# A hybrid decoder layer on one core: its prologue in another order

## The chip, the core and the metric

One core of a Trainium2 chip runs the whole program. The metric is device microseconds of one execution, from the chip. TensorE multiplies, VectorE and ScalarE do elementwise work, GpSimd fills constants, and SyncE issues the loads. Each engine works through its own list in order and waits for others at semaphores.

## What is computed

The reference is one layer of a decoder trunk over 256 tokens of 1024 channels: x is normalised, scaled and shifted by vectors made from the conditioning c, and multiplied by one wide matrix; three token mixers, gates and an output product follow. The change touches what stands ahead of the first products, the first two lines and the start of the third:

```python
shift, scale, gate = jnp.split(c @ w_ada[l] + b_ada[l], 3, axis=-1)
h = rmsnorm(x, norm_pre[l]) * (1.0 + scale[:, None]) + shift[:, None]
proj = h @ w_in[l] + b_in[l]
...
merged = (g[:, :, 0] * (y_a @ w_branch[l, 0]) + g[:, :, 1] * (y_b @ w_branch[l, 1])
          + g[:, :, 2] * (y_c @ w_branch[l, 2]))
out = merged @ w_out[l]
x = x + gate[:, None] * rmsnorm(out, norm_post[l])
```

## The kernel before

All is float32. A large product is made of three: each operand is split into a high part, rounded to the fast format (`hi`, a cast on ScalarE), and the rest (`lo`, a subtraction on VectorE); `hi*hi`, `hi*lo` and `lo*hi` are summed in PSUM. One weight tile is 128 x 1024; its split is one pass on ScalarE and one on VectorE.

**The prologue** (lines 325 to 500). `heat(n)` is n products of ones, whose result nobody reads. c, one value per partition and block of 128, is spread by eight products with an identity (`ps_cb`, line 348) into `cb`, 128 equal rows of 1024, which VectorE copies out of PSUM in two halves. x lies with tokens on partitions; ScalarE squares it with a running sum (`ss`), TensorE transposes it in 16 blocks (`ps_x`, `flip`), and the reciprocal root `r` of each token is refined on VectorE (`x_norm`), spread by two products (`ps_rx`) and read into `rrow` with a factor -0.5. xn is the transposed x times `rrow`. Its first half is made at once (`evac_x`), its second is copied out raw and multiplied by `rrow` later, at k = 3 and k = 5 of the loop.

**The wave** (the loop `for k in range(KT)`, from line 506). Step k holds channels 128 k to 128 k + 127. It needs the scale and the shift of these channels: `ada_dot` (line 491) is one pass of VectorE over 128 x 1024 of w_ada times `cb`, with a sum per partition, and there are two of them for each k. From them come the columns `a` and `b` (three small VectorE steps); ScalarE makes `h_hi` and `h_f` = a * xn + b, VectorE `h_lo`; the two weight tiles of the step are split; then TensorE runs 48 products of 128 x 256 into eight PSUM banks, which all eight steps share. A weight buffer is free for the load of step k+2 when VectorE is done with it: four buffers of 1 MB are in turn, two for each step.

**The order of the rest.** Every instruction is issued in the order in which the Python code makes it. After the wave this order is set by a planner, the class `Loom`: it charges each engine an estimated time for each instruction and lets generators (attention, convolution, gates) step in between the large products when its clock says that their operands are due. What is charged in the prologue therefore moves where later small work stands.

The names in the trace: `w` is the PSUM of the wave, `ps_f` and `ps_t` that of the later large products; `w_raw`, `w_hi`, `w_lo` the weight tile and its parts; `a_raw` a pair of rows of w_ada; `acol`, `bcol` the columns a and b. Nearly all instructions are recorded at line 174, the helper that issues them.

## Time and profile before

| | us |
|---|---|
| median of 3 runs (504.64 to 504.78) | 504.76 |
| the profiled execution | 505.05 |
| its span, first to last instruction | 503.3 |
| TensorE busy | 491.2 (98%) |
| VectorE busy | 433.3 (86%) |
| ScalarE busy | 306.7 (61%) |
| first product of the wave | 14.88 |
| first product after the wave | 62.65 |
| last large product | 495.56 |

The span is what the timeline covers; the rest of the execution's 505.05 us lies around it. TensorE's busy time is that of products that overlap, and their ends are modelled: where the pace of products matters, the distance from one start to the next is the better number. A float32 product of 128 columns leaves two records on TensorE, a transpose and a product of the fast format one. In the table of stages, the clock column says what share of full speed TensorE was granted.

### The profile page before, as it was taken

What the parts mean: (1) busy time and instruction counts of PE and PEld (TensorE: products, weight loads), DVE (VectorE), ACT (ScalarE), POOL (GpSimd) and SP (SyncE); (2) the same over time, 40 slices, a digit from 0 to 9 for tenths busy, and PEclk for the clock granted to TensorE, in tenths of its full rate; (3) what the DMA queues carried; (4) which work ended last, traced back from release to release, by engine and by line L of the source; (5) the groups of instructions that cost most, each with busy time, mean ns of one, the idle gap of its engine ahead of it and who ended that gap; (6) DMA issues with size and microseconds to landing.
All of it is one profiled execution on the core that took longest, in us unless ns stands there. A gap on an engine that the chain in (4) does not pass through costs nothing.

```text
span 503.3 us, 8482 instructions
## 1 busy us (share of the span) xinstructions
PE 491.2 (98%) x3221; PEld 436.5 (87%) x3221; DVE 433.3 (86%) x871; ACT 306.7 (61%) x520; POOL 7.3 (1%) x41
## 2 busy tenths in 40 slices
PE   7999999999999999999999999999999999999994
PEld 7999999789878989978899799997888788888883
DVE  3999889999999999999799997679998986656745
ACT  3646665335365868969767874666666834454442
POOL 5000000000000000000000000000000000000000
PEclk9999999999999999999999999999999999999998
DMA  8999965784787242443423526555277596655402
GB/s 309 331 364 331 411 267 198 302 318 180 262 316 255 85 169 85 168 139 114 167 85 133 191 72 233 178 195 205 98 300 312 189 349 247 236 215 195 168 0 83
DMA packets 18496, 106.38 MB, mean 211 GB/s; under 512 B 2188, under 2 KB 2584, under 8 KB 8344
## 3 DMA queue, kind: packets, MB, share of 16 engines
q1 hardware_dynamic: 18312, 105.82, 56.8%
q8 instruction: 25, 0.41, 0.3%
q14 instruction: 15, 0.12, 0.1%
q10 hardware_dynamic: 144, 0.03, 0.0%
HBM read 104.78 MB, written 1.06 MB: 210 GB/s over the span
## 4 chain that ended last, share of the span: by engine, by line
PE 87%; DVE 6%; ACT 2%; DMA 1%; issue 1%; POOL 1%; DVEq 0%; SPq 0%; POOLq 0%; ACTq 0%
PE ps_f L174 37%; PE ps_t L174 30%; PE ps_out L174 4%; PE ps_o L174 3%; DVE w_lo L174 2%; PE w L174 2%; PE ps_s L174 2%; DVE a_raw L174 2%; PE ps_c L174 2%; DMA w_raw<-in_wave_dram 1%; PE ps_p L174 1%; ACT w_hi L174 1%; PE ps_n L174 1%; PE ps_qk L174 1%; PE ps_cb L174 1%
## 5 line engine op out<-in xcount | busy, mean ns | idle before, releaser
L174 DVE TENSOR_TENSOR w_lo<-w_raw,w_hi 128x1024 fp32r<-128x1024 f32 x148 | 179.7, 1219 | 38.4 <-ACT w_hi L174 37.1
L174 ACT CAST w_hi<-w_raw 128x1024 fp32r<-128x1024 f32 x148 | 154.4, 1045 | 73.3 <-PE ps_t L174 52.5
L174 PE MATMUL ps_f<-h_hi,w_hi 128*128 128x256 f32 x512 | 130.8, 292 | 0.0
L174 PE MATMUL ps_f<-h_lo,w_hi 128*128 128x256 f32 x512 | 126.2, 283 | 0.0
L174 PEld LDWEIGHTS ps_f<-h_hi,w_hi 128*128 128x128 f32 x512 | 98.0, 191 | 2.4 <-issue 1.5
L174 PEld LDWEIGHTS ps_f<-h_lo,w_hi 128*128 128x128 f32 x512 | 98.1, 192 | 1.1 <-issue 0.7
L174 DVE SCALAR_TENSOR_TENSOR acc<-u,p_sb,acc 128x226 f32<-128x226 f32 (+28 forms) x232 | 92.8, 459 | 2.0 <-ACT acc L174 2.0
L174 PE MATMUL ps_f<-h_hi,w_lo 128*128 128x256 f32 x512 | 75.2, 287 | 0.0
L174 PEld LDWEIGHTS ps_f<-h_hi,w_lo 128*128 128x128 f32 x512 | 66.6, 191 | 2.5 <-issue 1.3
L174 PE MATMUL ps_t<-w_hi,h_hi 128*128 128x512 f32 x144 | 57.1, 397 | 0.2 <-DVE gs L174 0.2
L174 PE MATMUL ps_t<-w_hi,h_lo 128*128 128x512 f32 x144 | 56.2, 391 | 0.0
L174 PE MATMUL ps_t<-w_lo,h_hi 128*128 128x512 f32 x144 | 44.6, 391 | 0.0
L174 PEld LDWEIGHTS ps_t<-w_hi,h_hi 128*128 128x128 f32 x144 | 27.0, 188 | 6.8 <-issue 0.8
L174 ACT ACT_TABLE_LOAD x24 | 30.8, 1283 | 1.6 <-PEq L1493 1.2
L174 PEld LDWEIGHTS ps_t<-w_lo,h_hi 128*128 128x128 f32 x144 | 26.9, 188 | 5.7
L174 PEld LDWEIGHTS ps_t<-w_hi,h_lo 128*128 128x128 f32 x144 | 27.1, 188 | 5.3
L174 PE MATMUL w<-h_lo,w_hi 128*128 128x256 f32 x128 | 31.4, 283 | 0.0
L174 PE MATMUL w<-h_hi,w_lo 128*128 128x256 f32 x128 | 31.3, 282 | 0.0
L174 DVE SCALAR_TENSOR_TENSOR a_raw<-a_raw,cb 128x1024 f32<-128x1024 f32 x24 | 28.6, 1218 | 0.0
L174 PEld LDWEIGHTS w<-h_hi,w_lo 128*128 128x128 f32 x128 | 24.5, 191 | 0.0
L174 PEld LDWEIGHTS w<-h_lo,w_hi 128*128 128x128 f32 x128 | 24.5, 191 | 0.0
L174 ACT ACTIVATE pm<-pm,mx 128x16 f32<-128x16 f32 (+2 forms) x48 | 18.9, 397 | 2.9 <-DVE mx L174 2.9
(259 smaller groups left out, 695.0 us busy)
## 6 DMA issues: line engine op xcount, KB each, us to landing
w_raw<-in_wgrp_dram SPq DMA_DIRECT2D x50, 1024.0 KB, 5.1
w_raw<-in_wbr_dram SPq DMA_DIRECT2D x12, 1024.0 KB, 4.9
a_raw<-in_wada_dram SPq DMA_DIRECT2D x16, 512.0 KB, 7.0
w_raw<-in_wave_dram SPq DMA_DIRECT2D x16, 512.0 KB, 6.5
w_raw<-in_w_dram SPq DMA_DIRECT2D x8, 1024.0 KB, 4.8
a_raw<-in_wada_dram SPq DMA_DIRECT2D x4, 1024.0 KB, 4.8
w_raw<-in_wout_dram SPq DMA_DIRECT2D x4, 1024.0 KB, 4.8
vb_mg<-in_vbias_dram SPq DMA_DIRECT2D x3, 512.0 KB, 6.1
```

The lines of the kernel that those rows point to most:

```text
L174: inst = self.pin(fn(*args, **kw))
```

## The change

The prologue and the first two steps of the wave are written in another order, and some of their work is done in another way.

- The heats are 10 and 4 (before 5, 3 and 6).
- c is spread in two halves, each behind the two transposes of one half of x (blocks 0 and 1). VectorE copies one half of `cb`, ScalarE the other.
- The scale of k = 0 comes from TensorE: eight products of 128 x 128 blocks of w_ada, stored in another layout, with c as a broadcast column (`scale_mm`, `ps_a`), four before and four behind the spreading of r. `ada_dot` makes the shift of k = 0, as before.
- Blocks 2 to 7 of x are multiplied by r where they lie, with tokens on partitions (ScalarE one half, VectorE the other: 128 x 768 each), then transposed in 12 blocks, and read out with a factor -0.5 by ScalarE (`evac_late`, three passes). The two late multiplications at k = 3 and 5 are gone.
- In steps 0 and 1 `h_hi` is made on VectorE, the first weight tile is loaded and split in halves, and the scale dot of k = 1 stands in step 0.

```diff
@@ -61,7 +61,7 @@
 CATCH = 7
 BRANCHES = ((2, "c"), (0, "a"), (1, "b"))
 AHEAD = {2: ((0, 1), ()), 0: ((0,), (1,)), 1: ((0, 1), ())}
-HEAT = (5, 3, 6)
+HEAT = (10, 4)
 LEAD = 2
 BANKS = dict(mm=3, sd=3, ml=2)
 BIG, MID = 10, 3
@@ -342,12 +342,6 @@
     ident = const.tile([128, 128], F32, name="ident")
     make_identity(nc, ident)
     cb = const.tile([128, D], F32, name="cb")
-    ps_cb = [bank("ps_cb", "sd") for _ in range(2)]
-    for i in range(2):
-        for j in range(4):
-            mm(ps_cb[i][:, 128 * j:128 * j + 128], pc("c", 4 * i + j).broadcast_to([128, 128]), ident, True, True)
-        dve.tensor_copy(cb[:, 512 * i:512 * i + 512], ps_cb[i])
-        drop(ps_cb[i])
 
     def causal(o, rows_ge_cols, fill):
         pool.affine_select(out=o, in_=o, compare_op=OP.is_ge, fill=fill, base=0,
@@ -462,22 +456,34 @@
 
     xn = bigt("xn")
     xnf = xn.rearrange("p k s -> p (k s)")
-    ptr = [bank("ps_x", kind) for kind in ("mm", "sd", "ml", "ml")]
     ss, r, v = [work.tile([128, 2], F32, name=f"x{n}", bufs=1) for n in "srv"]
     rrow = const.tile([128, S], F32, name="rrow")
 
-    def evac_x(i):
-        dve.tensor_tensor(xn[:, 2 * i:2 * i + 2], ptr[i].rearrange("p (k s) -> p k s", k=2),
-                          rrow[:, None, :].broadcast_to([128, 2, S]), op=OP.mult)
+    def evac_late(i):
+        act.mul(xn[:, 2 * i:2 * i + 2], ptr[i].rearrange("p (k s) -> p k s", k=2), -0.5)
         drop(ptr[i])
+
+    def evac_x(i, j):
+        dve.tensor_tensor(xn[:, 2 * i + j], ptr[i][:, S * j:S * j + S], rrow, op=OP.mult)
+        if j:
+            drop(ptr[i])
+
+    ptr = [bank("ps_x", "ml")]
+    ps_cb = [bank("ps_cb", "sd") for _ in range(2)]
+
+    def flip_x(k, t):
+        flip(ptr[k // 2][:, 256 * (k % 2) + 128 * t:256 * (k % 2) + 128 * t + 128], x_sb[:, t, 128 * k:128 * k + 128])
 
     for t in range(2):
         act.activation(xnf[:, D * t:D * t + D], x_sb[:, t], AF.Square, accum_out=ss[:, t:t + 1])
-        for k in range(KT):
-            flip(ptr[k // 2][:, 256 * (k % 2) + 128 * t:256 * (k % 2) + 128 * t + 128],
-                 x_sb[:, t, 128 * k:128 * k + 128])
+        for k in range(2):
+            flip_x(k, t)
+        for j in range(4):
+            mm(ps_cb[t][:, 128 * j:128 * j + 128], pc("c", 4 * t + j).broadcast_to([128, 128]), ident, True, True)
+    dve.tensor_copy(cb[:, 0:512], ps_cb[0])
+    drop(ps_cb[0])
     act.activation(r, ss, AF.Sqrt, bias=eps, scale=1.0 / D)
-    heat(HEAT[1])
+    dve.tensor_scalar(v, ss, 1.0 / D, 1e-6, op0=OP.mult, op1=OP.add)
 
     def x_norm():
         dve.reciprocal(r, r)
@@ -487,6 +493,9 @@
         ps = bank("ps_rx")
         for t in range(2):
             mm(ps[:, 128 * t:128 * t + 128], r[:, t:t + 1].broadcast_to([128, 128]), ident, True, True)
+        late = [x_sb[:, t, 256:] for t in range(2)]
+        act.mul(late[0], late[0], r[:, 0:1])
+        dve.tensor_scalar(late[1], late[1], r[:, 1:2], None, op0=OP.mult)
         act.mul(rrow, ps[:, 0:S], -0.5)
         drop(ps)
 
@@ -502,52 +511,90 @@
     bcol = const.tile([128, 8], F32, name="bcol")
 
     kinds = [k for k in BANKS for _ in range(BANKS[k])]
-    banks = [bank(f"w0_{f}", kinds[f]) for f in range(8)]
+    raws_, wraws = [], []
     for k in range(KT):
-        raw = rawt([128, 2, D], "a_raw")
-        wraw = rawt([128, 2, 1024], "w_raw")
-        for i in range(2):
-            loom.load(nc.sync, raw[:, i], wada[k, :, i])
-        for i in range(2):
-            loom.load(nc.sync, wraw[:, i], wave0[k, :, 1024 * i:1024 * i + 1024])
-        if k == 0:
-            dve.tensor_scalar(v, ss, 1.0 / D, 1e-6, op0=OP.mult, op1=OP.add)
-        ada_dot(raw[:, 0], 8 + k)
-        if k == 0:
-            x_norm()
-        ada_dot(raw[:, 1], k)
-        if k == 0:
-            evac_x(0)
-        a, b = acol[:, k:k + 1], bcol[:, k:k + 1]
-        dve.scalar_tensor_tensor(a, adac[:, 8 + k:9 + k], 1.0, pc("b_ada", 8 + k), op0=OP.add, op1=OP.add)
-        dve.tensor_tensor(b, adac[:, k:k + 1], pc("b_ada", k), op=OP.add)
-        dve.tensor_tensor(a, a, pc("npre", k), op=OP.mult)
+        for j in range(k, k + 2 if k == 0 else k + 1 if k > 1 else k):
+            raw = rawt([128, 2, D], "a_raw")
+            wraw = rawt([128, 2, 1024], "w_raw")
+            raws_.append(raw)
+            wraws.append(wraw)
+            for i in range(2):
+                loom.load(nc.sync, raw[:, i], wada[j, :, i])
+            cuts = (0, 512, 1024, 2048) if j < 2 else (0, 1024, 2048)
+            flat = wraw.rearrange("p a b -> p (a b)")
+            for c0, c1 in zip(cuts, cuts[1:]):
+                loom.load(nc.sync, flat[:, c0:c1], wave0[j, :, c0:c1])
+        raw, wraw = raws_[k], wraws[k]
         hi = [ringt(his, [128, 1024], "w_hi", "hi", HIS, F32R) for _ in range(2)]
         lo = [ringt(los, [128, 1024], "w_lo", "lo", LOS, F32R) for _ in range(2)]
         h = h_f[:, k]
-        act.copy(hi[0], wraw[:, 0])
-        if 4 < k < CATCH:
+        a, b = acol[:, k:k + 1], bcol[:, k:k + 1]
+        if k == 0:
+            act.copy(cb[:, 512:], ps_cb[1])
+            drop(ps_cb[1])
+            ps_a = bank("ps_a")
+
+            def scale_mm(js):
+                for j in js:
+                    mm(ps_a[:, 0:128], raw[:, 0, 128 * j:128 * j + 128], pc("c", j).broadcast_to([128, 128]),
+                       j == 0, j == KT - 1)
+
+            scale_mm(range(4))
+            x_norm()
+            scale_mm(range(4, 8))
+            ada_dot(raw[:, 1], 0)
+            evac_x(0, 0)
+            mods = ps_a[:, 0:1], adac[:, 0:1]
+        else:
+            if k > 1:
+                ada_dot(raw[:, 0], 8 + k)
+            ada_dot(raw[:, 1], k)
+            mods = adac[:, 8 + k:9 + k], adac[:, k:k + 1]
+        dve.scalar_tensor_tensor(a, mods[0], 1.0, pc("b_ada", 8 + k), op0=OP.add, op1=OP.add)
+        dve.tensor_tensor(a, a, pc("npre", k), op=OP.mult)
+        dve.tensor_tensor(b, mods[1], pc("b_ada", k), op=OP.add)
+        if k == 0:
+            drop(ps_a)
+            ptr += [bank("ps_x", kind) for kind in ("sd", "ml", "sd")]
+            for t in range(2):
+                for j in range(2, KT):
+                    flip_x(j, t)
+            heat(HEAT[1])
+        if k < 2:
+            act.copy(hi[0][:, 0:512], wraw[:, 0, 0:512])
+            dve.tensor_scalar(h_hi[:, k], xn[:, k], a, b, op0=OP.mult, op1=OP.add)
+            act.copy(hi[0][:, 512:], wraw[:, 0, 512:])
+        else:
+            act.copy(hi[0], wraw[:, 0])
+            if 4 < k < CATCH:
+                act.copy(hi[1], wraw[:, 1])
+            act.activation(h_hi[:, k], xn[:, k], AF.Identity, scale=a, bias=b)
+        act.activation(h, xn[:, k], AF.Identity, scale=a, bias=b)
+        if k == 0:
+            evac_late(1)
+        if k < 5 or k >= CATCH:
             act.copy(hi[1], wraw[:, 1])
         if k == 0:
-            heat(HEAT[2])
-        act.activation(h_hi[:, k], xn[:, k], AF.Identity, scale=a, bias=b)
-        act.activation(h, xn[:, k], AF.Identity, scale=a, bias=b)
-        if k < 5 or k >= CATCH:
-            act.copy(hi[1], wraw[:, 1])
+            evac_late(2)
+            evac_late(3)
         if k == KT - 3:
             act.activation(warm, warm, AF.Sigmoid)
-        dve.tensor_tensor(lo[0], wraw[:, 0], hi[0], op=OP.subtract)
-        dve.tensor_tensor(h_lo[:, k], h, h_hi[:, k], op=OP.subtract)
+        if k < 2:
+            dve.tensor_tensor(lo[0][:, 0:512], wraw[:, 0, 0:512], hi[0][:, 0:512], op=OP.subtract)
+            dve.tensor_tensor(h_lo[:, k], h, h_hi[:, k], op=OP.subtract)
+            dve.tensor_tensor(lo[0][:, 512:], wraw[:, 0, 512:], hi[0][:, 512:], op=OP.subtract)
+            if k == 0:
+                evac_x(0, 1)
+        else:
+            dve.tensor_tensor(lo[0], wraw[:, 0], hi[0], op=OP.subtract)
+            dve.tensor_tensor(h_lo[:, k], h, h_hi[:, k], op=OP.subtract)
         if k == 0:
-            evac_x(1)
-            for i in range(2, 4):
-                act.copy(xn[:, 2 * i:2 * i + 2], ptr[i].rearrange("p (k s) -> p k s", k=2))
-                drop(ptr[i])
+            ada_dot(raws_[1][:, 0], 9)
         dve.tensor_tensor(lo[1], wraw[:, 1], hi[1], op=OP.subtract)
-        if k in (3, 5):
-            c = xn[:, k + 1:k + 3]
-            dve.tensor_tensor(c, c, rrow[:, None, :].broadcast_to([128, 2, S]), op=OP.mult)
         drop(raw, wraw)
+
+        if k == 0:
+            banks = [bank(f"w0_{f}", kinds[f]) for f in range(8)]
 
         def w0(f, j, w, x, start, stop):
             c = (f % 4) * 256 + j * 128
@@ -1431,6 +1478,7 @@
     a["xtok"] = cc(x.reshape(2, 128, D).transpose(1, 0, 2).reshape(128, 2 * D))
     wa = arr(w_ada)[0].T.reshape(3, 8, 128, D)
     pairs = [np.stack([wa[1, k], wa[0, k]], 1) for k in range(8)]
+    pairs[0] = np.stack([ktiles(wa[1, 0].T), wa[0, 0]], 1)
     pairs += [np.stack([wa[2, k], wa[2, k + 1]], 1) for k in range(0, 8, 2)]
     a["wada"] = cc(np.stack(pairs))
     o = OFF["ba"], OFF["bb"]
```

Where instructions stand now, in each engine's list. TensorE, from the start to the first products of the wave (`w`); before:

```order
L174 MATMUL ps_heat<-ones 128x128 x5
L174 MATMUL ps_cb<-ident,p_sb 128x128 x8
L174 MATMUL ps_x<-ident,x_sb 128x128 x16
L174 MATMUL ps_heat<-ones 128x128 x3
L174 MATMUL ps_rx<-ident,xr 128x128 x2
L174 MATMUL ps_heat<-ones 128x128 x6
L174 MATMUL w_0_194<-h_hi,w_hi 128x256 x2
```

The same place of the changed kernel (`ps_a` is the scale of k = 0):

```order
L174 MATMUL ps_heat<-ones 128x128 x10
L174 MATMUL ps_x<-ident,x_sb 128x128 x2
L174 MATMUL ps_cb<-ident,p_sb 128x128 x4
L174 MATMUL ps_x<-ident,x_sb 128x128 x2
L174 MATMUL ps_cb<-ident,p_sb 128x128 x4
L174 MATMUL ps_a<-p_sb,a_raw 128x128 x4
L174 MATMUL ps_rx<-ident,xr 128x128 x2
L174 MATMUL ps_a<-p_sb,a_raw 128x128 x4
L174 MATMUL ps_x<-ident,x_sb 128x128 x12
L174 MATMUL ps_heat<-ones 128x128 x4
L174 MATMUL w_0_257<-h_hi,w_hi 128x256 x2
```

The spreading of r (`ps_rx`) now stands ahead of 12 of the 16 transposes, and these stand between it and the wave.

VectorE, from the copy of `cb` to the first `w_lo`; before:

```order
L174 COPY cb<-ps_cb 128x512 x2
L174 TENSOR_SCALAR xv<-xs 128x2
L174 SCALAR_TENSOR_TENSOR a_raw,adac<-a_raw,cb 128x1024
L174 RECIPROCAL xr<-xr 128x2
L174 TENSOR_TENSOR xv<-xv,xr 128x2 x2
L174 SCALAR_TENSOR_TENSOR xr<-xv,xr 128x2
L174 SCALAR_TENSOR_TENSOR a_raw,adac<-a_raw,cb 128x1024
L174 TENSOR_TENSOR xn<-ps_x,rrow 128x512
L174 SCALAR_TENSOR_TENSOR acol<-adac,p_sb 128x1
L174 TENSOR_TENSOR bcol<-adac,p_sb 128x1
L174 TENSOR_TENSOR acol<-acol,p_sb 128x1
L174 TENSOR_TENSOR w_lo<-w_raw,w_hi 128x1024
```

The same place of the changed kernel:

```order
L174 COPY cb<-ps_cb 128x512
L174 TENSOR_SCALAR xv<-xs 128x2
L174 RECIPROCAL xr<-xr 128x2
L174 TENSOR_TENSOR xv<-xv,xr 128x2 x2
L174 SCALAR_TENSOR_TENSOR xr<-xv,xr 128x2
L174 TENSOR_SCALAR x_sb<-x_sb,xr 128x768
L174 SCALAR_TENSOR_TENSOR a_raw,adac<-a_raw,cb 128x1024
L174 TENSOR_TENSOR xn<-ps_x,rrow 128x256
L174 SCALAR_TENSOR_TENSOR acol<-ps_a,p_sb 128x1
L174 TENSOR_TENSOR acol<-acol,p_sb 128x1
L174 TENSOR_TENSOR bcol<-adac,p_sb 128x1
L174 TENSOR_SCALAR h_hi<-xn,acol,bcol 128x256
```

One of the two dots ahead of `acol` is gone, a pass over 768 columns of x stands ahead of the other, and `h_hi` is VectorE's.

TensorE behind the wave, at the end of a group of `ps_f` and the start of the next of `ps_t` (`ps_b`, `ps_c` and `ps_r` are small products of the gates and of the attention's compression); before:

```order
L174 MATMUL ps_b<-lf,upper 128x4
L174 MATMUL ps_b<-lf,ones 128x4
L174 MATMUL ps_b<-lf,upper 128x4
L174 MATMUL ps_f<-h_hi,w_lo 128x256 x8
L174 MATMUL ps_c_1002<-w_raw,ckb 32x256 x8
L174 MATMUL ps_r<-ident,acols 4x128 x2
L174 MATMUL ps_t<-w_hi,h_hi 128x512
L174 MATMUL ps_t<-w_hi,h_lo 128x512
```

The same place of the changed kernel:

```order
L174 MATMUL ps_f<-h_hi,w_lo 128x256 x8
L174 MATMUL ps_t<-w_hi,h_hi 128x512
L174 MATMUL ps_t<-w_hi,h_lo 128x512
L174 MATMUL ps_c_1020<-w_raw,ckb 32x256 x8
L174 MATMUL ps_r<-ident,acols 4x128 x2
```

The planner put `ps_c` and `ps_r` two large products later; such moves stand all through the rest of the program. ScalarE's list has 20 table loads in place of 24.

## Rows read from the trace of the kernel before

**Rows 1.** Stages: us, busy PE, PEld, DVE, ACT, POOL (records), clock, DMA share, GB/s.

```profile
0.00:14.88 14.88, 11.34 (x64) 10.89 (x64) 5.99 (x16) 6.05 (x11) 6.38 (x32) 1.00 0.86 326
14.88:62.65 47.77, 47.16 (x385) 46.44 (x385) 43.88 (x81) 29.04 (x40) 0.00 (x0) 1.00 0.97 356
62.65:280.00 217.35, 217.31 (x1615) 194.65 (x1613) 209.56 (x517) 145.13 (x299) 0.92 (x9) 1.00 0.52 190
```

**Rows 2.** Timeline, TensorE: start, us, engine, line, operation, shape, count [idle before <-releaser].

```profile
1.05 2.50 PE L174 MATMUL ps_heat<-ones 128*128 128x128 f32 x10 [1.05 <-POOL eps L322]
5.29 3.75 PE L174 MATMUL ps_cb<-ident,p_sb 128*128 128x128 f32 x16 [1.73 <-POOL mrow L856]
8.83 2.84 PE L174 MATMUL ps_x<-ident,x_sb 128*128 128x128 f32 x16
11.51 0.83 PE L174 MATMUL ps_heat<-ones 128*128 128x128 f32 x6
12.18 0.61 PE L174 MATMUL ps_rx<-ident,xr 128*128 128x128 f32 x4
...
14.88 0.39 PE L174 MATMUL w<-h_hi,w_hi 128*128 128x256 f32 x1 [0.75 <-ACT h_hi L174]
```

**Rows 3.** The same, two short pieces of the transposes.

```profile
9.05 1.70 PE L174 MATMUL ps_x<-ident,x_sb 128*128 128x128 f32 x7
...
10.86 0.71 PE L174 MATMUL ps_x<-ident,x_sb 128*128 128x128 f32 x5
```

**Rows 4.** Timeline, VectorE from 9 to 14.2 us.

```profile
9.80 1.23 DVE L174 SCALAR_TENSOR_TENSOR a_raw<-a_raw,cb 128x1024 f32<-128x1024 f32 x1
...
10.95 0.16 DVE L174 RECIPROCAL xr<-xr 128x2 f32<-128x2 f32 x1
...
11.62 1.22 DVE L174 SCALAR_TENSOR_TENSOR a_raw<-a_raw,cb 128x1024 f32<-128x1024 f32 x1
...
13.24 0.69 DVE L174 TENSOR_TENSOR xn<-ps_x,rrow 128x512 f32<-128x512 f32 x1 [0.40 <-ACT rrow L174]
13.85 0.15 DVE L174 SCALAR_TENSOR_TENSOR acol<-adac,p_sb 128x1 f32<-128x1 f32 x1
...
14.18 1.23 DVE L174 TENSOR_TENSOR w_lo<-w_raw,w_hi 128x1024 fp32r<-128x1024 f32 x1
```

**Rows 5.** Timeline, ScalarE from 5 to 14.3 us.

```profile
5.00 1.06 ACT L174 ACTIVATE xn<-x_sb 128x1024 f32<-128x1024 f32 x1 [2.26 <-DMA x_sb<-in_xtok_dram]
...
12.83 0.38 ACT L174 ACTIVATE rrow<-ps_rx 128x256 f32<-128x256 f32 x1 [5.03 <-PE ps_rx L174]
...
14.23 0.60 ACT L174 ACTIVATE h_hi<-xn,bcol,acol 128x256 fp32r<-128x256 f32 x1
```

**Rows 6.** Timeline, TensorE at the steps k = 4 and k = 6.

```profile
38.27 0.28 PE L174 MATMUL w<-h_hi,w_lo 128*128 128x256 f32 x1
39.02 0.39 PE L174 MATMUL w<-h_hi,w_hi 128*128 128x256 f32 x1 [0.47 <-ACT h_hi L174]
...
50.62 0.28 PE L174 MATMUL w<-h_hi,w_lo 128*128 128x256 f32 x1
51.04 0.51 PE L174 MATMUL w<-h_hi,w_hi 128*128 128x256 f32 x2
```

**Rows 7.** Timeline, VectorE, the rescaling ahead of k = 4 and one step.

```profile
35.09 0.69 DVE L174 TENSOR_TENSOR xn<-xn,rrow 128x512 f32<-128x512 f32 x1
35.69 1.22 DVE L174 SCALAR_TENSOR_TENSOR a_raw<-a_raw,cb 128x1024 f32<-128x1024 f32 x1
...
41.57 1.22 DVE L174 SCALAR_TENSOR_TENSOR a_raw<-a_raw,cb 128x1024 f32<-128x1024 f32 x1
```

**Rows 8.** Timeline, ScalarE, the second weight tile of k = 6.

```profile
49.43 1.05 ACT L174 CAST w_hi<-w_raw 128x1024 fp32r<-128x1024 f32 x1 [1.03 <-DMA w_raw<-in_wave_dram]
```

**Rows 9.** SyncE's loads of the second a_raw; time to landing (tile view).

```profile
4.03 1.47 SPq L204 DMA_DIRECT2D a_raw<-in_wada_dram  x2
...
DMA to landing us min/median/max: 9.1/9.1/9.2
```

## The prediction, made before the changed kernel ran

> **What bounds the kernel now.** I read the table by stage first [rows 1]. From 62.65 us on TensorE is busy 217.31 of 217.35 us, so nothing there shortens the run unless TensorE arrives earlier. Between 14.88 and 62.65 it is busy 47.16 of 47.77 us: that is the first product of the network, eight steps over k of 48 products each, which I call the wave. Before 14.88 it runs nothing that the reference asks for as a large product. So the change is worth two things: how much earlier the first wave product starts, and how many of the wave's small gaps close. The rest rides along, if the later order keeps TensorE fed; the 7.7 us behind the last product stay.
>
> Then the timeline of TensorE in the prologue [rows 2]: 64 records from 1.05 us, with a hole before the spreading of c (it starts at 5.29), and a hole of 0.75 us before the first wave product, which waits for h_hi. A product of 128 float32 columns leaves two records, a transpose one. Their pace has two values. The 16 records of ps_cb take 8.83 - 5.29 = 3.54 us, 0.221 each; seven transposes from 9.05 take 1.70 us with the tail of the last, and inside a run I take 0.213. The six heats at 11.51 take 0.67 us, 0.112 each. So TensorE starts at the lower of its levels (1.2 GHz) and has the higher (2.4 GHz) by 10.86; those seven are still slow, five from 10.86 take only 0.71 us [rows 3]. The rise lies near 10.65, amid transposes, after work without a hole since 5.29. (The clock column reads 1.00 from the start; here the pace must tell.)
>
> Then VectorE and ScalarE in the same stretch [rows 4, 5]. The dot with the scale row cannot start before c is spread (9.80), the one with the shift row stands behind the small norm steps (11.62), rrow comes at 12.83 because its products stand behind 16 transposes and three heats, then xn (13.24), a and b (13.85 to 14.18), and h_hi on ScalarE (14.23, 0.60 long). That chain sets 14.88.
>
> **The change part by part.**
>
> *TensorE's prologue.* It becomes 20 heat records (ten heats), 2 + 2 transposes, 16 of c, 16 new ones (ps_a, the scale of k=0 by eight products), 4 of rrow, 12 transposes, 8 heat records: 80 in place of 64. With ten heats the hole before 5.29 fills: ten records take 2.50 us, ten more 2.13, so the heats reach to about 5.5; the first half of x is there at 5.00 [rows 5]. From 1.05 on TensorE has no hole unless an operand is late. At 0.213 throughout, the first wave product could start at 1.2 + 80 x 0.213 = 18.2; if the clock rises at T, it is 9.6 + 0.474 T (each record after T takes 0.112 instead of 0.213). T is the unknown. Its ends: 10.65 as before (start 14.65), and 5.5, the end of the heats (12.2). No row shows a rise after so long an early run. I take 7.5, nearer to the early end, because the run without a hole starts 4.2 us earlier than before: start 13.15.
>
> *What the first product waits for, at T = 7.5.* The first half of c is spread at about 7.75. VectorE copies it (0.69, as the 512-wide step at 13.24 [rows 4]) to 8.5, one small step to 8.6, four small norm steps (11.62 - 10.95 = 0.67) to 9.3; r is there. ScalarE copies the other half of cb meanwhile. VectorE scales the second 768 columns of x: no row shows this operation; it is between the 512-wide step (0.69) and a 1024-wide one (1.23), I take 0.9: 10.2. The shift dot, 1.15 from start to start, to 11.35; xn of 256 columns, 0.4 by the 0.69 of 512, to 11.75; a and b, 14.18 - 13.85 = 0.33, to 12.1; h_hi, now on VectorE and 256 wide as well, 0.4, to 12.5. The dot with the scale row (1.15) and half of the first xn step are gone from this path. rrow does not hold it: its products stand behind four ps_a products (9.6 to 10.05), ScalarE scales its own part of x from 9.5 to 10.4 (a 1024-wide pass takes 1.06 [rows 5]) and writes rrow (0.38) by 10.8. w_hi, now in halves, is ready too. So h_hi is 0.6 us ahead of TensorE's own queue, whose last members are 12 transposes and 4 heats (20 x 0.112 = 2.2 us); those transposes wait for the scaled x (10.4) and are reached at about 10.95. The eight ps_a products cost TensorE 1.8 us and the four late heats 0.9 us, and both are on the path in this count. **Term 1: 14.88 to 13.15, 1.7 us gained** (bounds: 0.2 and 2.7).
>
> *The wave.* 384 products at 0.12 us are 46.1 us; it takes 47.77. The largest holes are at 39.02 (0.75 us from the product before, start to start, in place of 0.12) and 51.04 (0.42) [rows 6]. The first comes from the rescaling of xn on VectorE (0.69, 0.60 of it in the step) [rows 7]: with x scaled ahead, both rescalings go. The second comes from a weight tile that lands late, ScalarE waits for it to 49.43 [rows 8]: this stays. The other steps start about 0.1 late each, since the loop of VectorE and ScalarE takes 41.57 - 35.69 = 5.88 us [rows 7] and 48 products take 5.76. Does the new start outrun VectorE? After h_hi it has two half w_lo and h_lo (14.05), xn (14.45), the scale dot of k=1, brought forward, (15.6; its row of w_ada lands 9.1 us after 4.03, at 13.1 [rows 9]), w_lo (16.75), one dot (17.9), a, b and h_hi (18.65); TensorE is at k=1 at 18.9. At k=2 it is 24.6 against 24.7. From there the 5.88 loop is again 0.1 longer than TensorE's step. So 0.6 is sure, 0.1 to 0.2 in each of the first two steps likely, the full 1.6 not. **Term 2: 0.9 us gained** (0.5 to 1.5).
>
> *Costs that I put at nothing.* Three loads in place of two for k=0 and 1: all are issued far ahead of their bytes, and the same bytes pass. evac_late on ScalarE: three 512-wide passes, half of 1.06 us each, beside TensorE's first step, the last done near 15.3, when the sixth bank is needed at 13.15 + 3.1 = 16.3; without that cover up to 0.5. Banks that the transposes hold are otherwise free by then.
>
> *The later order.* The planner times the rest by what it charged so far, so small products and ScalarE's work stand elsewhere among the large ones. The work is the same, apart from 20 table loads in place of 24. TensorE idles 0.04 us of 217 after the wave [rows 1], so there is nothing to win, and VectorE is busy 209.56 of those 217.35, so there is something to lose. Bounds: 0 and about 2 us lost; I take 0.
>
> *Sum.* The profiled run took 505.05 us (span 503.3, 1.75 around it). 505.05 - 1.7 - 0.9 = 502.45. The median, 504.76, lies 0.29 lower: **502.15**.
>
> **The rivals.**
>
> *A. The start hardly moves.* T stays near 10.65, or VectorE's path is late because cb is spread at the lower clock: the start is 14.65 and only the wave's gain remains, up to 1.4 then, since VectorE gets ahead: 503.2 to 504.1. For it: the clock rose only at 10.65 before, though the first heats ran at 1.05. Against: what then ran without a hole from 5.29 now does so from 1.05. Chance 0.14.
>
> *B. The later part takes it back.* VectorE at 96% is next to TensorE; where the new order brings TensorE to a product whose operand VectorE has not made, it waits. 1 to 2.6 us back: 503.2 to 504.8. Against: VectorE's prologue shortens as well, by a dot, two rescalings and half of the cb copies. Chance 0.12.
>
> *C. The clock is still low when the wave should start.* Then the 80 records are a loss: there are 16 more than before, and by the formula each us of delay of the rise costs 0.47 us. With the wave's 1.4 the gain is used up at a start of 16.3, so T = 14.1; from T = 16.2 on it is slower by over 0.2%, and with no rise before the wave it starts at 18.2, 3.4 us later: 504.76 + 3.4 - 1.4 = 506.8, and wave products at the lower pace on top. For it: the last records before the wave are 12 transposes and only 8 of heat, where 6 + 4 + 12 stood after the transposes. Against: [rows 3], the clock rose while transposes ran. The Trainium skill, "TensorE: Matmul & The Clock Gate", section "Part 4: PE-mode transpose", says that a transpose does not count as activity in the way that lets TensorE have its full clock. By that page 16 of the 80 records do nothing for the clock and the last 12 may let it go, which is this rival; the trace, in which it rose with eight transposes just behind it and more running, does not support it but does not exclude it, as products stood before them. Chance 0.05.
>
> *D. More than forecast.* T near 5.5 and the whole 1.6 us of the wave: below 500.9. Chance 0.05.
>
> **How the numbers follow.** The forecast, 500.9 to 503.2, has 0.64; A 0.14, B 0.12, C 0.05, D 0.05. The range 500.7 to 504.2 takes in A and most of B, and leaves out C, a part of D and the end of B. About 0.2% (1.0 us) is what a measurement can tell from no change: the line lies at 503.75. Faster: 0.64 + 0.05 + half of A and B, 0.82. Same: the other half, 0.13. Slower: C, 0.05.
>
> **What would show it.** In the profile after: heats, transposes and c without a hole from 1.05, and the pace falling to 0.112 near 7.5 (term 1); the first wave product near 13.15 behind heat, not behind h_hi; the next steps near 18.9 and 24.7 (term 2), no hole at the fifth step, the wave's end near 60.0 in place of 62.65; after it, TensorE idle under 0.5 us up to its last product. It is wrong if the pace stays at 0.213 past 10.65 (A, C), if the first product waits for VectorE (the 768-wide step or the dot mis-sized), or if TensorE shows idle time behind VectorE after the wave (B).

## The result, and the profile after

The changed kernel takes 502.11 us in the median of four runs (501.86 to 502.75), the kernel before 504.75 in four beside it (504.64 to 504.78): a ratio of 0.9947, 95% interval 0.9934 to 0.9961. It is 2.6 us faster; the forecast was 502.15. Further down, one run of e8_x_unscaled, its profiled one (1253.91 us), and one of e11_half_ada (985.67) ran far slower throughout than the others of their kernels; all medians are of the other runs.

| | before | after |
|---|---|---|
| the profiled execution, us | 505.05 | 502.75 |
| pace of TensorE doubles at | 10.73 | 5.0 |
| first product of the wave | 14.88 | 12.49 |
| length of the wave | 47.77 | 47.15 |
| first product after the wave | 62.65 | 59.64 |
| from there to the last large product | 432.91 | 433.58 |

The profiled executions differ by 2.30: 2.39 gained at the start, 0.62 in the wave, 0.67 lost behind it, and 0.04 around them. After's profiled run is the slowest of its four. The three stages of after, in the columns of [rows 1]:

```profile
0.00:12.49 12.49, 11.05 (x81) 10.86 (x81) 5.18 (x16) 8.34 (x15) 6.38 (x32) 1.00 0.83 297
12.49:59.64 47.15, 47.11 (x387) 46.43 (x386) 42.55 (x81) 28.14 (x39) 0.00 (x0) 1.00 1.00 388
59.64:277.00 217.36, 216.81 (x1612) 194.32 (x1611) 211.94 (x525) 140.29 (x296) 0.92 (x9) 1.00 0.51 190
```

DMA engines were busy 0.97 of the wave before and are busy 1.00 of it now. Behind the wave TensorE idles 0.55 us (217.36 less 216.81) where it idled 0.04. TensorE's prologue, in the columns of [rows 2]:

```profile
1.05 4.37 PE L174 MATMUL ps_heat<-ones 128*128 128x128 f32 x20 [1.05 <-POOL eps L322]
5.26 0.38 PE L174 MATMUL ps_x<-ident,x_sb 128*128 128x128 f32 x2
5.47 1.06 PE L174 MATMUL ps_cb<-ident,p_sb 128*128 128x128 f32 x8
...
8.03 1.16 PE L174 MATMUL ps_a<-p_sb,a_raw 128*128 128x128 f32 x8 [0.39 <-DMA a_raw<-in_wada_dram]
9.03 0.61 PE L174 MATMUL ps_rx<-ident,xr 128*128 128x128 f32 x4
9.47 1.06 PE L174 MATMUL ps_a<-p_sb,a_raw 128*128 128x128 f32 x8
10.37 1.47 PE L174 MATMUL ps_x<-ident,x_sb 128*128 128x128 f32 x12
11.68 1.06 PE L174 MATMUL ps_heat<-ones 128*128 128x128 f32 x8
12.49 0.96 PE L174 MATMUL w<-h_hi,w_hi 128*128 128x256 f32 x6
```

The heats fill the time from 1.05 to 5.26, and their pace changes inside them: 17 records up to 4.7 us lie 0.213 apart, the records from 5.03 on 0.11. The first wave product starts behind heat, with no wait of its own. VectorE ahead of it, as in [rows 4]:

```profile
8.53 0.62 DVE L174 TENSOR_SCALAR x_sb<-x_sb,xr 128x768 f32<-128x768 f32 x1
9.37 1.23 DVE L174 SCALAR_TENSOR_TENSOR a_raw<-a_raw,cb 128x1024 f32<-128x1024 f32 x1 [0.21 <-DMA a_raw<-in_wada_dram]
...
10.52 0.42 DVE L174 TENSOR_TENSOR xn<-ps_x,rrow 128x256 f32<-128x256 f32 x1
...
11.30 0.41 DVE L174 TENSOR_SCALAR h_hi<-xn,acol,bcol 128x256 fp32r<-128x256 f32 x1
```

`h_hi` ends at 11.71, 0.78 before TensorE comes to it. TensorE at k = 4, which answers to [rows 6]:

```profile
35.81 0.28 PE L174 MATMUL w<-h_hi,w_lo 128*128 128x256 f32 x1
36.03 0.62 PE L174 MATMUL w<-h_hi,w_hi 128*128 128x256 f32 x3
```

The distance there is 0.22; before it was 0.75. What TensorE waits for behind the wave (engine, tile, releaser: us in all, times, longest):

```profile
PE ps_c L174 <- DMA w_raw<-in_w_dram: 0.4, 1, 0.4
PE ps_t L174 <- DVE w_lo L174: 0.3, 1, 0.3
PE ps_t L174 <- DVE gs L174: 0.2, 1, 0.2
PE ps_b L174 <- DVE lf L174: 0.2, 1, 0.2
```

The kernel before has the two `ps_t` rows alone; `ps_c` and `ps_b` are new, 0.6 us together, nearly all of the 0.67. Whether the new order brings them is looked at below.

### The profile page after: what moved, and what is told of

Its sections match the earlier page's. It is cut to its first block, busy times and chain, and to the rows that moved or that the text cites. A ratio compares the mean times of both kernels' runs of the same rounds, so it can differ in the third digit from the quotient of the medians.

```text
span 501.0 us, 8523 instructions
## 1 busy us (share of the span) xinstructions
PE 491.0 (98%) x3237; PEld 436.4 (87%) x3237; DVE 431.8 (86%) x871; ACT 303.1 (61%) x519; POOL 7.3 (1%) x41
## 4 chain that ended last, share of the span: by engine, by line
PE 83%; DVE 11%; DMA 2%; issue 2%; ACT 1%; SPq 0%; DVEq 0%; ACTq 0%
PE ps_f L174 30%; PE ps_t L174 28%; PE w L174 9%; PE ps_out L174 4%; DVE w_lo L174 4%; DVE acc L174 3%; PE ps_o L174 3%; PE ps_s L174 2%; PE ps_p L174 1%; DMA a_raw<-in_wada_dram 1%; DMA w_raw<-in_w_dram 1%; PE ps_qk L174 1%; PE ps_n L174 1%; PE ps_c L174 1%; DVE cm L174 1%
## 5 line engine op out<-in xcount | busy, mean ns | idle before, releaser
L174 DVE TENSOR_TENSOR w_lo<-w_raw,w_hi 128x1024 fp32r<-128x1024 f32 (+1 forms) x150 | 180.0, 1205 | 40.6 <-ACT w_hi L174 39.2
L174 ACT CAST w_hi<-w_raw 128x1024 fp32r<-128x1024 f32 (+1 forms) x150 | 154.9, 1034 | 81.9 <-PE ps_t L174 53.3
L174 PE MATMUL ps_t<-w_hi,h_hi 128*128 128x512 f32 x144 | 58.2, 404 | 0.2 <-DVE gs L174 0.2
L174 DVE SCALAR_TENSOR_TENSOR a_raw<-a_raw,cb 128x1024 f32<-128x1024 f32 x23 | 27.4, 1218 | 0.2 <-DMA a_raw<-in_wada_dram 0.2
```

Of the source, the lines that this page charges most:

```text
L174: inst = self.pin(fn(*args, **kw))
```

## Experiments

A ratio is to the kernel before on the same chip, in 9 to 17 runs per group (medians 504.69 to 504.86). An interval reaches about 0.6 us to either side, so smaller differences of two medians are open unless the traces show their place. There is one profile of each kernel. The kernels ran in three groups, each on its own chip: e0 to e3; e7, e8, e10 and e11; e5, e6, e12 and e13.

| | median us | ratio, interval | first product | wave |
|---|---|---|---|---|
| e0_after | 502.28 | 0.9944 (0.9932 to 0.9956) | 12.57 | 46.77 |
| e1_pin | 502.12 | 0.9942 (0.9930 to 0.9954) | 12.46 | 47.08 |
| e2_heat5 | 503.01 | 0.9959 (0.9945 to 0.9973) | 14.43 | 46.24 |
| e3_before_heat10 | 503.42 | 0.9973 (0.9963 to 0.9983) | 13.84 | 47.61 |
| e7_scale_vector | 502.59 | 0.9951 (0.9936 to 0.9965) | 12.76 | 47.63 |
| e8_x_unscaled | 503.04 | 0.9961 (0.9947 to 0.9975) | not seen | not seen |
| e11_half_ada | 503.86 | 0.9981 (0.9971 to 0.9991) | 12.46 | 48.62 |
| e10_swap_no_heat | 501.58 | 0.9931 (0.9917 to 0.9945) | 11.69 | 47.48 |
| e12_abc | 502.32 | 0.9946 (0.9933 to 0.9960) | 12.24 | 47.38 |
| e13_loop | 501.99 | 0.9944 (0.9930 to 0.9957) | 11.57 | 48.74 |
| e5_heat_transposes | 502.41 | 0.9951 (0.9938 to 0.9965) | 12.48 | 47.06 |
| e6_heat_products | 502.48 | 0.9952 (0.9938 to 0.9965) | 12.32 | 46.98 |

**The changed kernel again, and its later order taken back.** e0_after is the changed kernel. e1_pin gives the planner, at the end of the wave, the state that it had there in the kernel before, so all that follows stands in the order of before:

```diff
+    shift = 58974.1566666667 - loom.free["pe"]
...
+    loom.free = dict(pe=58974.1566666667, act=53898.17333333332, dve=55182.83999999998, dma=47323.44666666666)
```

> The changed kernel once more, as the base of this group. If its gain is what the first runs showed, 501.9 to 502.3 us, with the first wave product at 12.4 to 12.6 and the wave's end near 59.6. If the clock's rise moves from run to run, the first wave product moves with it, by up to 1 us, and the time as well.

> The changed kernel with the later order of the kernel before: at the end of the wave the planner's state is set to the one it had there, so that every engine's list behind the wave is that of before. Theory: the new order costs what the profile shows, 433.58 us from the wave's end to the last product in place of 432.91, so this one is 0.5 to 0.7 us faster than the changed kernel, 501.4 to 501.7. Rival: the 0.67 us are chance of one execution (one wait for a load is 0.4 of them), then it is the same within 0.2 us.

These two traces look like the theory: from the wave's end to the last large product e0_after takes 433.56 us, with 0.6 of wait at `ps_b`, and e1_pin 432.71, with neither `ps_b` nor `ps_c` in its waits. But the medians differ by only 0.16, which is the rival's case, and the later profiles speak for the rival too. All later kernels keep the order of before behind the wave, and five of their nine profiles (that of e8_x_unscaled left aside) have the new waits all the same. In e12_abc and e5_heat_transposes:

```profile
PE ps_b L174 <- DVE lf L174: 0.4, 1, 0.4
```

```profile
PE ps_c L174 <- DMA w_raw<-in_w_dram: 0.6, 1, 0.6
```

That stretch takes 433.16 us in e6_heat_products, 433.34 in e12_abc, 433.62 in e5_heat_transposes, 433.64 in e11_half_ada and 434.29 in e3_before_heat10; it takes 432.88 to 433.06 in e2_heat5, e7_scale_vector, e10_swap_no_heat and e13_loop. So the waits come and go under one order, and that the new order costs 0.67 is not shown. All later kernels but e3_before_heat10 build on e1_pin.

**The heats alone.** e2_heat5 is e1_pin with `HEAT = (5, 4)`. e3_before_heat10 is the kernel before with `HEAT = (10, 3, 6)`.

> As e1_pin, with five early heats in place of ten. Theory (the unbroken run from 1.05 is what brings the clock up early): the pace of 0.213 us lasts far longer, the first wave product starts between 13.5 and 14.8, and half of that comes back in the wave since VectorE is then ahead: 0.8 to 1.8 us slower than e1_pin. Rival (the order of the prologue is what counts, the clock hardly does): the first wave product within 0.3 us of e1_pin's, the time within 0.2.

> The kernel before with ten early heats in place of five and nothing else, later order as before. Theory: the heats alone give most of the earlier start: c is spread by about 7.1, the dots end at 9.0 and 10.9, the first wave product starts at 12.6 to 12.9 in place of 14.88; the hole at the fifth step (0.6) stays, so 502.3 to 502.9. Rival: the old chain (two dots, rrow behind 16 transposes, h_hi on ScalarE) holds the start at 14 or later, 504 or more.

In e2_heat5 the pace doubled at 10.72, its first product started 1.97 us later than e1_pin's, and the time rose by 0.89. That answers to rival A's late rise, and the theory of the rise held. In e3_before_heat10 it doubled at 7.2, and heats alone brought 1.4 of the 2.6 us; the start, 13.84, is later than expected, and 503.42 lies between the ranges of theory and rival. Its profiled run is its slowest (505.22), and it shows how an early start is lost again. Steps k = 0 to 7 start 1.04 to 1.30 ahead of the kernel before. Then ScalarE waits for a weight tile:

```profile
53.86 1.05 ACT L174 CAST w_hi<-w_raw 128x1024 fp32r<-128x1024 f32 x1 [3.68 <-DMA w_raw<-in_wave_dram]
```

That cast starts no earlier than before (53.78). Two `w_lo` later VectorE is only 0.13 ahead (58.74 against 58.87), and when TensorE comes to the next small product that needs VectorE, it waits (its waits behind the wave):

```profile
PE ps_b L174 <- DVE lf L174: 1.1, 1, 1.1
...
PE ps_c L174 <- DMA w_raw<-in_w_dram: 0.3, 1, 0.3
```

That is rival B of the prediction, here with the later order unchanged: VectorE and the transfers were not earlier when TensorE was, and the new order is not needed for it.

**Parts undone.** e7_scale_vector: the scale of k = 0 by a dot on VectorE, `ps_a` gone. e8_x_unscaled: x goes raw into its late transposes, and the rescalings stand at k = 3 and 5 again.

```diff
-            scale_mm(range(4))
...
+            ada_dot(raw[:, 0], 8)
```

```diff
-        act.mul(late[0], late[0], r[:, 0:1])
-        dve.tensor_scalar(late[1], late[1], r[:, 1:2], None, op0=OP.mult)
...
+        if k in (3, 5):
+            c = xn[:, k + 1:k + 3]
+            dve.tensor_tensor(c, c, rrow[:, None, :].broadcast_to([128, 2, S]), op=OP.mult)
```

> As e1_pin, and one part undone: the scale of k=0 is a dot product on VectorE again (1.15 us more on VectorE ahead of the first product), and the eight products into ps_a (1.8 us on TensorE) are gone. Theory of the prediction: TensorE's own queue ends near 11.0 now, and VectorE's chain becomes the one that ends last: xn, acol and h_hi come 1.15 later than e1_pin's, h_hi ends at 12.7 to 12.9, so the first product moves from 12.46 to 12.7 to 12.9 and the time to 502.3 to 502.6. Rival (transfers set the wave's end): the first product moves as said, but the wave gets shorter by as much, since its late tiles come when they came: wave end at 59.5, 502.0 to 502.2. By both the eight products save much less than the 1.8 us that they cost.

> The changed kernel with the later order of the kernel before (as e1_pin), and one part undone: x goes into its late transposes unscaled, so VectorE's 768-wide step and ScalarE's twin of it are gone from the start and the two 512-wide rescalings of the tiles k=4,5 and k=6,7 stand in the steps k=3 and k=5 again. The prediction's theory (the hole of 0.6 at k=4 was that rescaling): the wave starts within 0.1 of e1_pin's 12.46, a hole of 0.4 to 0.6 is back ahead of k=4, the wave is 47.4 to 47.7 long and the time 0.2 to 0.6 above e1_pin's 502.12: 502.3 to 502.7. Rival (the weight transfers set the wave's length now, DMA engines at 1.00 of their time in it): VectorE waits for late tiles anyway, the rescalings fall into those waits, the wave stays 47.0 to 47.2 long, 502.0 to 502.2.

e7_scale_vector came as the theory had it. Its first wave product, on TensorE:

```profile
12.76 1.07 PE L174 MATMUL w<-h_hi,w_hi 128*128 128x256 f32 x7 [0.76 <-DVE h_hi L174]
```

TensorE is done with its heat early and waits 0.76 for `h_hi`: the eight products save 0.3 us at the start, although they cost TensorE 1.8. The wave did not make up for it: it is 47.63 long, with one step (k = 4) of 6.45, in which ScalarE waits 2.17 for a weight tile. The time is 0.47 above e1_pin's, less than two medians resolve. e8_x_unscaled is 0.9 above e1_pin, more than the 0.2 to 0.6 expected, and the rival (502.2 at most) fell. No trace of it can be set beside the others, so where the extra lies stays open. The spreading of c in two halves and the new form of the first two steps were not undone by themselves.

**What sets the wave now.** I suspected the transfers. e11_half_ada loads only half of each `a_raw` tile from k = 2 on and goes over that half twice; its output is therefore another.

```diff
-                loom.load(nc.sync, raw[:, i], wada[j, :, i])
+                loom.load(nc.sync if j < 2 else Half(nc.sync), raw[:, i], wada[j, :, i])
...
+                half_dot(raw[:, 0], 8 + k)
+                half_dot(raw[:, 1], k)
```

> As e1_pin, with half of the modulation weights' bytes left out from k=2 on: of each of the two 512 KB tiles a_raw only the first half is loaded, and VectorE does two 512-wide steps on that half in place of one 1024-wide step (about 0.1 us more of VectorE for each), so what it computes is not the reference's; all other work is the same. Of some 1.5 MB that each step of the wave reads, 0.5 MB are gone. Theory (transfers set the wave's length: DMA engines at 1.00, ScalarE waiting 11.4 us for w_raw in it): ScalarE's waits for w_raw fall below 2 us, the wave gets as short as e2_heat5's 46.24 in spite of the two dots' extra time, and ends at 58.6 to 58.8: 501.1 to 501.4. Rival (the order of the engines' work sets it): the wave stays 47.0 to 47.2, 502.0 to 502.2.

The 1.5 MB are what is left of a step's reads; the whole is 2 MB, four tiles of 512 KB. My theory fell: it is slower, 503.86. The wave of e11_half_ada, in the columns of the stages:

```profile
12.46:61.08 48.62, 47.12 (x388) 46.31 (x387) 44.44 (x104) 27.75 (x39) 0.00 (x0) 1.00 0.85 303
```

The transfers' share fell from e1_pin's 1.00 to 0.85 and ScalarE's waits for `w_raw` from 11.4 to 2.3 us, yet the wave grew by 1.54. One step of e1_pin on VectorE shows why:

```profile
31.69 1.23 DVE L174 TENSOR_TENSOR w_lo<-w_raw,w_hi 128x1024 fp32r<-128x1024 f32 x1 [0.52 <-ACT w_hi L174]
32.84 1.22 DVE L174 SCALAR_TENSOR_TENSOR a_raw<-a_raw,cb 128x1024 f32<-128x1024 f32 x1
...
33.98 1.22 DVE L174 SCALAR_TENSOR_TENSOR a_raw<-a_raw,cb 128x1024 f32<-128x1024 f32 x1
...
35.13 0.15 DVE L174 SCALAR_TENSOR_TENSOR acol<-adac,p_sb 128x1 f32<-128x1 f32 x1
35.31 0.16 DVE L174 TENSOR_TENSOR acol<-acol,p_sb 128x1 f32<-128x1 f32 x1
35.39 0.15 DVE L174 TENSOR_TENSOR bcol<-adac,p_sb 128x1 f32<-128x1 f32 x1
35.46 1.22 DVE L174 TENSOR_TENSOR w_lo<-w_raw,w_hi 128x1024 fp32r<-128x1024 f32 x1
...
37.64 1.23 DVE L174 TENSOR_TENSOR w_lo<-w_raw,w_hi 128x1024 fp32r<-128x1024 f32 x1 [0.52 <-ACT w_hi L174]
```

and on ScalarE:

```profile
32.76 1.05 ACT L174 CAST w_hi<-w_raw 128x1024 fp32r<-128x1024 f32 x1 [1.10 <-DMA w_raw<-in_wave_dram]
35.58 0.60 ACT L174 ACTIVATE h_hi<-xn,bcol,acol 128x256 fp32r<-128x256 f32 x1 [1.76 <-DVE bcol L174]
36.08 0.59 ACT L174 ACTIVATE h_f<-xn,bcol,acol 128x256 f32<-128x256 f32 x1
36.58 1.04 ACT L174 CAST w_hi<-w_raw 128x1024 fp32r<-128x1024 f32 x1
```

VectorE's small steps release `h_hi`; behind it ScalarE makes `h_f` and the second `w_hi`; for this VectorE waits 0.52 before its second `w_lo`, then come two dots and the next small steps. That is a loop of 5.95 us, longer than TensorE's 48 products (5.76). In e11_half_ada four short dots take the place of two (first and last shown):

```profile
32.44 1.23 DVE L174 TENSOR_TENSOR w_lo<-w_raw,w_hi 128x1024 fp32r<-128x1024 f32 x1 [0.51 <-ACT w_hi L174]
33.58 0.69 DVE L517 SCALAR_TENSOR_TENSOR a_raw<-a_raw,cb 128x512 f32<-128x512 f32 x1
...
35.65 0.69 DVE L517 SCALAR_TENSOR_TENSOR a_raw<-a_raw,cb 128x512 f32<-128x512 f32 x1
...
36.53 0.15 DVE L174 TENSOR_TENSOR bcol<-adac,p_sb 128x1 f32<-128x1 f32 x1
```

From 33.58 to the small steps' end they take 0.40 more than from 32.84 in e1_pin, and the steps k = 2, 3 and 4 take 6.36 in place of 5.95: what is added to the loop is added to the step. The loop sets these steps, not the bytes. The wave of e2_heat5, which starts 1.97 later, has no hole:

```profile
14.43:60.68 46.25, 46.25 (x388) 46.20 (x387) 42.47 (x80) 27.83 (x39) 0.00 (x0) 1.00 1.00 375
```

There TensorE comes late enough for its operands in every step. VectorE's loop is no shorter for it; its first small steps of k = 3 and k = 4 in e2_heat5 lie 5.95 apart, while TensorE's own steps take 5.76:

```profile
30.29 0.16 DVE L174 SCALAR_TENSOR_TENSOR acol<-adac,p_sb 128x1 f32<-128x1 f32 x1
...
36.24 0.15 DVE L174 SCALAR_TENSOR_TENSOR acol<-adac,p_sb 128x1 f32<-128x1 f32 x1
```

So TensorE does not set the loop's length.

**The start, and the loop.** e10_swap_no_heat drops the four late heats and puts VectorE's second `w_lo` of k = 0 ahead of the dot of k = 1, so that its load is asked for earlier. e12_abc puts the three small steps in the order of before. e13_loop is e10 and e12 together, and moves the next dot into VectorE's wait.

```diff
-            heat(HEAT[1])
...
+        dve.tensor_tensor(lo[1], wraw[:, 1], hi[1], op=OP.subtract)
         if k == 0:
             ada_dot(raws_[1][:, 0], 9)
-        dve.tensor_tensor(lo[1], wraw[:, 1], hi[1], op=OP.subtract)
```

```diff
         dve.scalar_tensor_tensor(a, mods[0], 1.0, pc("b_ada", 8 + k), op0=OP.add, op1=OP.add)
+        dve.tensor_tensor(b, mods[1], pc("b_ada", k), op=OP.add)
         dve.tensor_tensor(a, a, pc("npre", k), op=OP.mult)
-        dve.tensor_tensor(b, mods[1], pc("b_ada", k), op=OP.add)
```

```diff
+        if k in EARLY:
+            load_step(k + 1)
+            ada_dot(raws_[k + 1][:, 0], 9 + k)
         dve.tensor_tensor(lo[1], wraw[:, 1], hi[1], op=OP.subtract)
...
-            if 4 < k < CATCH:
+            if 3 < k < CATCH:
```

> As e1_pin, without the four late products on ones (0.9 us of TensorE's queue ahead of the wave), and with VectorE's second low half of k=0 (lo[1]) put ahead of the first dot product of k=1, so that the weight tile of k=2 is asked for 1.15 us earlier. Theory (start carries through): h_hi ends near 11.7, the first product starts at 11.7 to 11.9 (0.6 to 0.8 earlier than e1_pin's 12.46), k=2 at 23.5 to 23.8 (24.33), and the wave ends at 58.8 to 59.0: 501.3 to 501.6. Rival (transfers set the wave's end): the same start, but ScalarE's waits for w_raw grow by as much and the wave ends at 59.3 to 59.5: 501.9 to 502.2. Second rival (the clock): without the four products the granted clock falls ahead of the first products of the wave, they run at half pace for a time, and the wave ends after 60: over 502.8.

> As e1_pin, with VectorE's three one-element steps of each k in the order of the kernel before again (scale, shift, scale times npre, in place of scale, scale times npre, shift). Theory, from e11_half_ada: what sets the steps k=2 to k=5 is the loop between VectorE and ScalarE (two dots, the three small steps, ScalarE's h_hi, h_f and second w_hi, for which VectorE's second w_lo waits 0.52), not the transfers; with the shift last, and two dependent steps back to back, the loop takes 5.95 in e1_pin, and 5.88 in the kernel before. So the steps k=2 to k=5 go from 5.95 to 5.88, the wave gets 0.2 to 0.3 shorter, 501.8 to 501.95. Rival (transfers or TensorE set these steps): 5.95 stays, 502.0 to 502.2.

> As e10_swap_no_heat, with the loop between VectorE and ScalarE opened: in the steps k=1 to 3 VectorE does the first dot of k+1 where it waited 0.52 for ScalarE's second w_hi (ahead of its second w_lo), at k=4 ScalarE makes the second w_hi ahead of h_hi, and the three small steps stand in the order of the kernel before. Theory (the loop sets the steps): VectorE's work of a step is some 5.4, so TensorE's own 5.76 sets them; k=2 stays near 23.9, the steps after it go to 5.76 to 5.85, the wave ends at 58.4 to 58.8 (59.17 in e10) and the time is 500.9 to 501.3 (501.58). Rival (transfers): the loads that wait for the second w_lo are asked for 0.6 later, tiles come later, the wave ends at 59.1 to 59.4, 501.5 to 501.8.

e10_swap_no_heat has the lowest median, 501.58. Its last transposes and first products:

```profile
10.13 1.47 PE L174 MATMUL ps_x<-ident,x_sb 128*128 128x128 f32 x12
11.69 1.07 PE L174 MATMUL w<-h_hi,w_hi 128*128 128x256 f32 x7
```

The four heats were not needed: the pace holds without them, so the rival of the clock fell. The start is 0.77 earlier than e1_pin's, k = 1 only 0.53 and k = 2 only 0.40; from there to the wave's end (0.37) nearly nothing more is lost. So half of the gain goes in the first two steps, ahead of those that the loop sets. VectorE holds k = 1, whose `h_hi` ends only 0.12 earlier (17.62 against 17.74), and a weight tile holds k = 2; its cast on ScalarE:

```profile
22.33 1.05 ACT L174 CAST w_hi<-w_raw 128x1024 fp32r<-128x1024 f32 x1 [3.58 <-DMA w_raw<-in_wave_dram]
```

It starts 0.22 earlier than in e1_pin (22.55), though the tile was asked for 1.27 earlier (14.57 against 15.84). The time is 0.5 below that of the changed kernel, with intervals that overlap.

In e12_abc the loop is as short as the theory said. VectorE's last small steps of k = 3 and k = 4:

```profile
29.65 0.15 DVE L174 TENSOR_TENSOR acol<-acol,p_sb 128x1 f32<-128x1 f32 x1
...
35.53 0.15 DVE L174 TENSOR_TENSOR acol<-acol,p_sb 128x1 f32<-128x1 f32 x1
```

They lie 5.88 apart, and TensorE's steps from k = 3 are 5.87 and 5.89. But k = 2 came 6.52 after k = 1 in this run, where the weights of k = 1 and 2 were there about 0.35 later than in e1_pin (22.89 against 22.55 for the latter), and the median, 502.32, shows no gain: 0.2 cannot be told here.

e13_loop gained nothing over e10_swap_no_heat: its median is 0.41 higher, less than the medians resolve, and its profiled execution (502.88) is its slowest. In that profile the loop is open for two steps, VectorE's first small steps of k = 2, 3 and 4 lie 5.29 and 5.27 apart, and TensorE's step k = 2 takes 5.84; but the steps k = 1 (6.69) and k = 3 (6.83) lose more, by transfers. On VectorE at k = 1, and on ScalarE ahead of k = 4:

```profile
19.80 1.23 DVE L174 SCALAR_TENSOR_TENSOR a_raw<-a_raw,cb 128x1024 f32<-128x1024 f32 x1 [0.83 <-DMA a_raw<-in_wada_dram]
...
20.95 1.22 DVE L174 TENSOR_TENSOR w_lo<-w_raw,w_hi 128x1024 fp32r<-128x1024 f32 x1
```

```profile
34.06 1.05 ACT L174 CAST w_hi<-w_raw 128x1024 fp32r<-128x1024 f32 x1 [3.13 <-DMA w_raw<-in_wave_dram]
```

The dot brought forward waits for its own tile, the second `w_lo` behind it (20.95; in e12_abc it starts at 20.13) frees its buffer later, and the loads that wait for such buffers go out at 22.20 and 27.48, against 20.32 and 26.61 in e10_swap_no_heat. The weights of k = 4 are there at 34.06, against 32.54, and k = 4 starts at 36.94, against 35.84.

**Do transposes raise the clock?** e5_heat_transposes and its twin put 20 transposes, or ten products, of the identity in the place of the ten products on ones.

```diff
-    heat(HEAT[0])
...
+    for _ in range(20):
+        flip(ps_h[:, 0:128], ident)
```

```diff
-    heat(HEAT[0])
...
+    for _ in range(10):
+        mm(ps_h[:, 0:128], ident, ident, True, True)
```

> As e1_pin, with the ten early products on ones replaced by 20 transposes of the identity, which take TensorE as long at either pace and start when the identity is there, near 1.7. The rule of the Trainium skill (TensorE: Matmul & The Clock Gate, Part 4: PE-mode transpose) is that transposes don't raise the clock: then it rises only after the c products that follow, at 8 to 11, the first product starts at 13.5 to 14.5 and the time is 502.9 or more, as e2_heat5 (rise 10.72, 503.01). Rival (transposes count as products do): rise at 4.5 to 7.5, start near 12.5, 502.0 to 502.4, as its twin e6_heat_products.

> The twin of e5_heat_transposes: ten products of the identity by itself in place of the ten on ones, at the same place and from the same moment, near 1.7. Both theories: rise at 5 to 7.5, first product at 12.4 to 12.7, 502.0 to 502.4. If this one is as late as e5, what counted there was the later begin of the activity, not its kind.

TensorE in e5_heat_transposes, where every record of the first row is a transpose:

```profile
1.70 3.87 PE L174 MATMUL ps_heat<-ident 128*128 128x128 f32 x20 [1.70 <-POOL ident masks.py:199]
5.40 0.38 PE L174 MATMUL ps_x<-ident,x_sb 128*128 128x128 f32 x2
5.62 1.06 PE L174 MATMUL ps_cb<-ident,p_sb 128*128 128x128 f32 x8
```

20 transposes from 1.70 to 5.40 are 0.185 each in the mean, between the two paces of the prediction: the pace doubled at 4.75, when TensorE had run nothing but transposes, and the products of c that follow are at 0.111 from the first. The twin doubled at 5.3, and the starts and times of the two are those of the rival (12.48 and 12.32, 502.41 and 502.48). So here transposes raised the clock as products did, in one profile of each, and the ground that the page gave rival C is not borne out. This differs from the rule that the prediction weighed for C, that of the Trainium skill, "TensorE: Matmul & The Clock Gate", section "Part 4: PE-mode transpose"; the measurement decides.

## Why the prediction was right, point by point

- **T** was put at 7.5 with bounds 5.5 and 10.65. It was 5.0, 6.53 and 5.45 in the three profiles of this prologue (after, e0_after, e1_pin): earlier than taken, twice earlier than the bound, and another in each execution. That TensorE, kept busy from 1.05 on, gets the higher clock far earlier than 10.73 was right; the size was a guess.
- **The formula** gives 11.97 for T = 5.0; 12.49 came. What it left out is that TensorE waits for the row of w_ada: `ps_a` starts at 8.03 behind a wait of 0.39 for `a_raw`, and the 40 records from there at 0.1115 are the 4.46 us to 12.49. An earlier rise than these brings little more: the starts of the three are 12.49, 12.57 and 12.46, though the rise moves by 1.5.
- **Term 1** is the term that was mis-sized: 1.7 forecast, 2.39 came, inside its bounds.
- **VectorE ahead of TensorE**, 0.65 forecast, 0.78 measured. The 768-wide step took 0.62, not 0.9: I had put it between two operations with two tensor inputs, and this one has one. The Trainium skill, "VectorE: DVE Perf Modes", section "The perf-mode tier table (the rule you actually need)", says that such an operation on float32 in SBUF runs at twice the pace of one with two tensors. This row points the same way: midway between the two-tensor rows of 512 (0.68) and 1024 (1.22) columns lies 0.95. `h_hi`, also of one tensor, does not: 0.41 for 256 columns, where two tensors take 0.42. The error was harmless: the wait of 0.21 for `a_raw` ahead of the dot took part of it, and the path had room.
- **The eight `ps_a` products and four late heats on the path**: right, TensorE's queue was what ended last. e7_scale_vector shows what the former bring at the start, 0.3 us; e10_swap_no_heat shows that the latter could go.
- **Term 2**, 0.9 forecast: 0.62 in after, 1.00 in e0_after, 0.69 in e1_pin. The hole at k = 4 went, and e8_x_unscaled, where the rescalings come back, loses 0.9. That the loop takes longer than TensorE's step was in the prediction, but at 5.88; the changed order of the small steps, which it did not cost, makes 5.95 of it.
- **The later order at nothing** was the step that failed, within its bounds: 0.67 was lost in after and 0.65 in e0_after, by waits at `ps_b` and `ps_c`. It is rival B on a smaller scale, and B's sign was there: 0.55 us of idle by 277 us, where under 0.5 was set. The cause that B names, the new order, is not shown, since the order of before has the same waits in five profiles of ten; e3_before_heat10 shows late weight tiles behind one of them.
- The forecast is so near by luck, because its errors cancel: 0.69 too little for term 1, and 0.28 and 0.67 too much for the others. By the profiled executions it is 0.3 off (502.45 against 502.75), and the medians close that.

Of the 2.6 us, e3_before_heat10 puts 1.4 down to the heats in the old order, e2_heat5 0.9 in the new one. That they are worth less where more of the chain behind them has been shortened would fit, but 0.5 is less than the medians resolve.

## What to carry to other kernels

A prologue that runs at the lower clock gets shorter by early work that fills TensorE, since the rise comes earlier, but only until the landing of an operand ends last (here a row of w_ada at 8.03); look for that landing before adding more. Where TensorE alone starts earlier, part of the gain is lost again as soon as it needs VectorE or a weight tile that is not earlier too. A stage in which TensorE is 99% busy can still be set by a loop of two other engines that is 2% longer than TensorE's step: add up the loop from its rows, and count the one-element steps and their order too. When such a loop is opened by a swap, look at which buffer the swapped instruction frees, and which load waits for it.
